# Scores of one pair of heads and values of the pair ahead, issued in one visit of TensorE between the projections

## The chip, the cores and the metric

The kernel runs on one core of one Trainium2 chip. The metric is device time in microseconds (us), the median of three executions. Five engines work side by side, each through its own queue in order: TensorE (PE; its weight loads are shown apart as PEld), VectorE (DVE), ScalarE (ACT), GpSimd (POOL) and SyncE (SP), which issues the DMAs.

## The reference

Two layers over 256 tokens of 1024 channels, float32. Each layer projects the normalised input to queries, keys, values and gates of 16 heads of 64 channels; six heads attend causally, six with a dilated pattern (here a mask and a weight for each pair of tokens), four attend to 256 memory rows; the gated results are projected back and added. Cut to what matters:

```python
def hybrid_layer(x, mem, norm_g, w_in, w_out, mem_norm_g, w_mem_kv, qk_g):
    proj = jnp.einsum('btd,de->bte', rms_norm(x, norm_g), w_in)
    a_q, a_k, a_v, a_g, b_q, b_k, b_v, b_g, m_q, m_g = jnp.split(proj, cuts, axis=-1)
    m_k, m_v = jnp.split(jnp.einsum('bmd,de->bme', rms_norm(mem, mem_norm_g), w_mem_kv), 2, axis=-1)
    oa = moba_attention(rope(rms_norm(a_q)), rope(rms_norm(a_k)), a_v)     # causal, 6 heads
    ob = dilated_attention(rope(rms_norm(b_q)), rope(rms_norm(b_k)), b_v)  # 6 heads
    om = memory_attention(rms_norm(m_q), rms_norm(m_k), m_v)               # 4 heads
    y = jnp.concatenate([oa * jax.nn.silu(a_g), ob * jax.nn.silu(b_g), om * jax.nn.silu(m_g)], axis=-1)
    return x + jnp.einsum('bte,ed->btd', y, w_out)

def memory_attention(q, k, v):
    s = jnp.einsum('bhqd,bhkd->bhqk', q, k) * (HEAD_DIM ** -0.5)
    return jnp.einsum('bhqk,bhkd->bhqd', jax.nn.softmax(s, axis=-1), v)
```

## The kernel before

**Projections.** Every weight is loaded in float32 (`raw`), split into a high part (`hi`, ACT, L449) and a rest (`lo`, DVE, L450), and multiplied by the split input (`xmh`, `xml`) in three products that accumulate in the PSUM tiles `acc` (`products`, L145). The order of a layer is: memory keys and values, memory queries, memory gates; then for the dilated and after it for the causal heads queries, keys, values, gates; then the output projection, whose inputs are the split results `yT0` and `yT1` (tile names with a number: yT_253 is yT0 of layer 0, yT_254 is yT1). A split buffer is free again when the matmuls that read it are done (five buffers), so a late `hi` cast waits for PE.

**Attention of a pair of heads** (`pair_of_heads`, L300, and `head`, L345). Heads go in pairs, eight pairs in a layer: two of memory, three dilated, three causal. A pair passes through these steps on PE, each a short visit between the projections' matmuls:

- four transposes of queries and keys (`wk<-ident,qn`, `wk<-ident,kn`), copied by ACT to `qkT` (L307);
- the scores, `wk<-qkT` (L319): four matmuls in float32 that contract over 64 channels, the two heads in the two halves of the array's rows;
- the softmax off PE: DVE takes the maximum (L351 for memory pairs, L358 with the mask for the others: `nm`, `pr`), ACT the exponentials (L353, L360), DVE the reciprocal (L364), ACT the scaling (L366);
- six or eight transposes of the probabilities (`wk<-ident,pr`, L374), copied by ACT to `pT` (L377);
- the values, `o<-pT,v` (L336): four matmuls that write 64 channels each, the two heads in the two halves of the array's columns;
- then DVE multiplies by the gate (`y`, L341), ACT and DVE split it into `yT0` and `yT1` (L562, L563).

**What sets the order.** The program is written once by Python; PE's order is pinned. Each pair is a generator that yields an estimated delay, and `poll` (L124), which is called between steps of the projections, continues every task whose time has come on an estimated PE clock. Pairs take their scores in order (`live["s"] == me`, L311) and their values in order (`live["v"] == me`, L327); three `wk` tiles and one `o` tile in PSUM are shared. At the output projection `finish` (L136, used in L653) moves the estimated clock on until the result that a step needs has been issued, whatever is or isn't left to put in between. ACT's and DVE's unpinned instructions are placed by the tile framework, which also inserts the semaphores; each engine then goes through its queue in order.

**The end of a layer.** The products of rows e = 1 and 2 of the output projection are held back (L657) and come last, in 24 matmuls that finish one PSUM bank after the other (L663 to L665). Row e = 2 is the last causal pair, the eighth.

Of the kernel before, what the change touches and what calls it, by code (L numbers as in the profile page):

```python
# [10 lines left out]
F32 = mybir.dt.float32  # L11
# [5 lines left out]
P = 128  # L17
T = 256
# [3 lines left out]
HD = 64  # L22
# [9 lines left out]
D_NORM, D_MEM, D_QK, D_SOFTMAX, D_PT, D_EVAC = 8, 1, 2.5, 5, 2.5, 4  # L32
D_FIRST_MEM, D_NEXT_MEM, D_PAIR, D_HEAD = 1, 3, 2, 1
WARM = 7

WHOLE = 2
NEG = -1e30
# [29 lines left out]
def hybrid_kernel(ctx: ExitStack, tc: tile.TileContext, x, mem, mem_t, gains, w_in, w_out, w_mem_kv, qk_g, const, out):  # L67
# [6 lines left out]
    o_p = ctx.enter_context(tc.tile_pool(name="op", bufs=O_BUFS, space=bass.MemoryType.PSUM))  # L74

    def work():
        return wk_p.tile([P, 512], F32, tag="wk", name="wk")
# [22 lines left out]
    clock, tasks = [0.0], []  # L100

    def pe(ins, us):

        tc.keep_in_program_order(ins)
        clock[0] += us

    def mm(out, a, b, start=True, stop=True, shared=False):
        n = b.shape[-1]
        us = 0.02 if shared else max(0.107, n / 2400) if b.dtype == F32R else max(0.214, n / 600)
        pe(nc.tensor.matmul(out, a, b, start=start, stop=stop), us)  # L110

    def transpose(out, a):
        pe(nc.tensor.transpose(out, a, ident), 0.109)  # L113
# [3 lines left out]
    def keep_warm(n):  # L117

        for _ in range(n):
            pe(nc.tensor.matmul(warm[:, 0:P], blank, blank, start=True, stop=True), 0)  # L120

    keep_warm(WARM)

# [9 lines left out]
    def spawn(gen, delay):  # L133
        tasks.append([clock[0] + delay, gen])
# [6 lines left out]
    def until(cond):  # L141
        while not cond():
            yield 0.3
# [125 lines left out]
    def normed(accs, n, dsts, tables, scale=None):  # L269
# [25 lines left out]
                                            op=ALU.mult))  # L295
        return rest

    live = dict(pr=0, pT=0, o=0, heads=0, pairs=0, s=0, t=0, v=0)

    def pair_of_heads(qn, kn, pair, masks, v, gate, ready, finished):  # L300

        ps = work()
        for t in range(NT):
            transpose(ps[:, t * P:(t + 1) * P], qn[:, t, pair * P:(pair + 1) * P])
            transpose(ps[:, 256 + t * P:256 + (t + 1) * P], kn[:, t, pair * P:(pair + 1) * P])
        qkT = sp.tile([P, 2, T], F32, tag="qkT", name="qkT", bufs=SLOTS)
        nc.scalar.copy(qkT.rearrange("p c t -> p (c t)"), ps)  # L307
        me = live["pairs"]
        live["pairs"] += 1
        yield D_QK  # L310
        yield from until(lambda: live["s"] == me and live["pr"] + 2 <= PR_BUFS)  # L311
        live["s"] += 1
        live["pr"] += 2
        scores = [work() for _ in range(2)]
        spans = [slice(0, 2 * P), slice(2 * P, 4 * P)] if masks is None else [slice(0, P), slice(P, 3 * P)]
        for t in range(NT):
            for j in range(2):
                q, k = (qkT[j * HD:(j + 1) * HD, c] for c in range(2))
                mm(scores[j][:, spans[t]], q[:, t * P:(t + 1) * P], k[:, 0:spans[t].stop - spans[t].start])  # L319
        pTs = []  # L320
        for j in range(2):
            rest = head(2 * me + j, scores[j], spans, masks, pTs)
            spawn(rest, next(rest))
        yield D_SOFTMAX
        yield from until(lambda: len(pTs) == 2)
        yield D_PT
        yield from until(lambda: live["v"] == me and live["o"] < O_BUFS and max(ready.values()) <= clock[0])  # L327
        live["v"] += 1
        live["o"] += 1
        o = o_p.tile([P, T], F32, tag="o", name="o")  # L330
        late = slice(0, T) if masks is None else slice(P, T)
        n = 2 * T if masks is None else T + P
        for t, to in ((0, slice(0, T)), (1, late)):
            for j in range(2):
                h = 2 * pair + j
                mm(o[j * HD:(j + 1) * HD, to], v[:, t, h * HD:(h + 1) * HD], pTs[j][:, t * T:n if t else T],  # L336
                   start=t == 0, stop=t == 1, shared=j)
        live["pT"] -= 2
        yield 0.6
        y = sp.tile([P, T], F32, tag="y", name="y", bufs=2)  # L340
        nc.vector.scalar_tensor_tensor(y, o, 0.5, gate[:, pair], op0=ALU.mult, op1=ALU.mult)  # L341
        live["o"] -= 1
        finished(y)
# [50 lines left out]
    for i, (l, c) in enumerate(order):  # L394
        if c in e_rows:
            e0, n = e_rows[c]
            units += [(i, a, min(2, n - a), D) for a in range(0, n, 2)]
        else:
            n = 512 if c == "mkv" else in_cols[c][1]
# [101 lines left out]
    for l in range(DEPTH):  # L501
# [51 lines left out]
        def head_tiles(n, nv):  # L553
            return [sp.tile([P, NT, n], F32, tag=c, name=c, bufs=1) for c in ("qn", "kn")] + [
                sp.tile([P, NT, nv], F32, tag="v", name="v", bufs=2),
                sp.tile([P, n // P, T], F32, tag="gate", name="gate", bufs=2)]
# [3 lines left out]
        def finished(y, e, yT=yT, done=done):  # L560
            done.add(e)
            nc.scalar.copy(yT[0][:, e], y)  # L562
            nc.vector.tensor_tensor(yT[1][:, e], y, yT[0][:, e].bitcast(F32), op=ALU.subtract)  # L563

        def start_heads(pairs, e0, qn, kn, masks, v, gate, ready, delay=D_NORM):
            for pair in range(pairs):
                spawn(pair_of_heads(qn, kn, pair, masks, v, gate, ready,
                                    lambda y, e=e0 + pair: finished(y, e)), delay + D_PAIR * pair)
# [3 lines left out]
        v = kv[:, :, 256:512]  # L572
# [45 lines left out]
        for kind, e0 in ((2, 3), (0, 0)):  # L618
            if kind == 2:
                masks = [cst[:, C_DIL:C_DIL + 128], cst[:, C_DIL + 128:C_DIL + 384]]  # L620
            else:
                masks = [cst[:, C_CAUSAL + 128:C_CAUSAL + 256], cst[:, C_CAUSAL:C_CAUSAL + 256]]
# [3 lines left out]
            qn, kn, v, gate = head_tiles(384, 384)  # L626
# [76 lines left out]
```

## Time and profile before

| | us |
|---|---|
| median of 3 runs (lowest to highest) | 292.39 (292.35 to 293.44) |
| the profiled execution, its own time | 292.14 |
| its span, first to last instruction | 290.3 |
| PE busy in the span | 284.8 (98%) |
| DVE, ACT busy | 205.0, 199.9 |

The page gives PE at 98% of the span and the granted clock of TensorE at 1.00 throughout. The ends of matmuls are modelled and overlap the next, so the reader should go by the distance from one start to the next start, not by the durations. In the section of rows below, "x8" behind the scores or the values are eight hardware matmuls: each float32 matmul of the program is two.

### The profile page before, as it was taken

To read this page: it belongs to the slowest core of one execution; us is meant where nothing else is said; L and a number is where in the kernel's file an instruction comes from. 1 tells how busy PE (TensorE), PEld (TensorE's weight loads), DVE (VectorE), ACT (ScalarE), POOL (GpSimd) and SP (SyncE) were. 2 spreads that over 40 slices of the span, in tenths; PEclk is the share of its full clock that TensorE was granted. 3 is DMA by queue.
4 is the path that set the end of the run, shared out by engine and by line. 5 is a ranking of instruction groups with operands and counts; after the bars stand their busy time and mean duration, and the time that the engine had idled before them with its cause. 6 is when DMAs were issued, how large, how long until landed. Compare 5 with 4: busy or idle time off the path is not lost.

```text
span 290.3 us, 4967 instructions
## 1 busy us (share of the span) xinstructions
PE 284.8 (98%) x1810; PEld 250.0 (86%) x1810; DVE 205.0 (71%) x458; ACT 199.9 (69%) x445; POOL 54.3 (19%) x72
## 2 busy tenths in 40 slices
PE   8999999999999999999999999999999999999994
PEld 5689999889989999877788999989899899987773
DVE  1798999793677996764676577979655699765313
ACT  2899677876789638985366555868578865797600
POOL 0002983210003220000020069503000113000000
PEclk9999999999999999999999999999999999999999
DMA  7999674627335236548025818360913624830003
GB/s 240 377 365 369 216 222 159 167 54 271 111 94 162 72 123 248 213 142 289 3 73 183 255 72 229 135 183 0 325 26 107 232 68 151 310 108 19 3 0 145
DMA packets 32793, 47.33 MB, mean 163 GB/s; under 512 B 1280, under 2 KB 27648, under 8 KB 32768
## 3 DMA queue, kind: packets, MB, share of 16 engines
q1 hardware_dynamic: 32336, 46.22, 48.6%
q10 hardware_dynamic: 432, 0.79, 0.8%
q8 instruction: 14, 0.23, 0.3%
q14 instruction: 11, 0.09, 0.1%
HBM read 45.96 MB, written 1.05 MB: 162 GB/s over the span
## 4 chain that ended last, share of the span: by engine, by line
PE 93%; DMA 3%; DVE 1%; ACT 0%; POOL 0%; SPq 0%; issue 0%; DVEq 0%
PE acc L110 76%; PE wk L113 8%; PE wk L110 5%; PE o L110 5%; DMA x_sb<-in_x_dram 2%; DMA raw<-in_w_mem_kv_dram 1%; DVE xn L491 0%; ACT xn L160 0%; POOL r L155 0%; SPq L428 0%; DVE x_sb L669 0%; SPq L98 0%; DVEq L699 0%; DVE ms L154 0%; PE o L113 0%
## 5 line engine op out<-in xcount | busy, mean ns | idle before, releaser
L450 DVE TENSOR_TENSOR lo<-raw,hi 128x768 fp32r<-128x768 f32 (+1 forms) x91 | 96.8, 1088 | 30.7 <-ACT hi L449 30.7
L449 ACT CAST hi<-raw 128x768 fp32r<-128x768 f32 (+1 forms) x91 | 84.0, 937 | 31.2 <-PE acc L110 21.9
L110 PE MATMUL acc<-hi,xmh 128*128 128x384 f32 (+2 forms) x252 | 67.0, 348 | 0.3 <-ACT hi L449 0.3
L110 PE MATMUL acc<-lo,xmh 128*128 128x384 f32 (+2 forms) x252 | 63.5, 335 | 0.0
L110 PE MATMUL acc<-hi,xml 128*128 128x384 f32 (+2 forms) x252 | 63.5, 335 | 0.0
L155 POOL TENSOR_TENSOR hrs<-ms,mhalf 128x6 f32<-128x6 f32 (+1 forms) x24 | 30.2, 1262 | 118.0 <-DVE ms L154 117.5
L110 PEld LDWEIGHTS acc<-hi,xmh 128*128 128x128 f32 x252 | 42.5, 189 | 5.8 <-issue 3.0
L110 PEld LDWEIGHTS acc<-lo,xmh 128*128 128x128 f32 x252 | 45.0, 188 | 1.2
L110 PEld LDWEIGHTS acc<-hi,xml 128*128 128x128 f32 x252 | 44.9, 188 | 1.2
L110 PE MATMUL acc<-hi,yT 128*128 128x512 f32 x128 | 41.0, 402 | 0.0
L110 PE MATMUL acc<-xmh,hi 128*128 128x256 f32 x128 | 29.7, 293 | 0.0
L110 PE MATMUL acc<-xml,hi 128*128 128x256 f32 x128 | 28.4, 283 | 0.0
L110 PE MATMUL acc<-xmh,lo 128*128 128x256 f32 x128 | 28.3, 283 | 0.0
L110 PEld LDWEIGHTS acc<-hi,yT 128*128 128x128 f32 x128 | 23.0, 188 | 4.8 <-issue 0.7
L360 ACT ACTIVATE pr<-pr,nm 128x128 f32<-128x128 f32 (+1 forms) x48 | 21.3, 446 | 7.7 <-DVE nm L358 7.6
L366 ACT ACTIVATE pr<-pr,rinv 128x128 f32<-128x128 f32 (+1 forms) x64 | 25.8, 462 | 0.0
L110 PE MATMUL acc<-lo,yT 128*128 128x512 f32 x64 | 25.0, 391 | 0.0
L110 PEld LDWEIGHTS acc<-xmh,hi 128*128 128x128 f32 x128 | 20.9, 191 | 0.7 <-issue 0.7
L110 PEld LDWEIGHTS acc<-xml,hi 128*128 128x128 f32 x128 | 21.0, 191 | 0.0
L110 PEld LDWEIGHTS acc<-xmh,lo 128*128 128x128 f32 x128 | 21.0, 191 | 0.0
L377 ACT COPY pT<-wk 128x384 f32<-128x384 f32 (+1 forms) x32 | 15.4, 503 | 6.1 <-PE wk L113 6.1
L358 DVE CUSTOM_DVE_ANT_0 pr<-wk,cst 128x128 f32<-128x128 f32 (+1 forms) x48 | 14.3, 353 | 3.3 <-PE wk L110 3.3
(79 smaller groups left out, 353.1 us busy)
## 6 DMA issues: line engine op xcount, KB each, us to landing
raw<-in_w_in_dram SPq DMA_DIRECT2D x24, 768.0 KB, 5.2
raw<-in_w_in_dram SPq DMA_DIRECT2D x7, 1024.0 KB, 5.8
raw<-in_w_out_dram SPq DMA_DIRECT2D x6, 1024.0 KB, 4.9
raw<-in_w_in_dram SPq DMA_DIRECT2D x6, 512.0 KB, 3.8
raw<-in_w_out_dram SPq DMA_DIRECT2D x4, 512.0 KB, 4.2
raw<-in_w_mem_kv_dram SPq DMA_DIRECT2D x2, 1024.0 KB, 5.1
raw<-in_w_mem_kv_dram SPq DMA_DIRECT2D x2, 512.0 KB, 6.9
x_sb<-in_x_dram SPq DMA_DIRECT2D x2, 512.0 KB, 7.1
```

The lines of the kernel that those rows point to most:

```text
L110: pe(nc.tensor.matmul(out, a, b, start=start, stop=stop), us)
L113: pe(nc.tensor.transpose(out, a, ident), 0.109)
L155: pin(nc.gpsimd.tensor_tensor(dst, ms, mhalf[:, :n], op=ALU.pow))
L358: nc.vector.tensor_tensor_reduce(out=pr[:, spans[t]], in0=s[:, spans[t]], in1=masks[t], scale=-1.0, scalar=3e38, op0=ALU.add, op1=ALU.min, ...
L360: nc.scalar.activation(pr[:, spans[t]], pr[:, spans[t]], AF.Exp, scale=-1.0, bias=nm[:, t:t + 1], accum_out=sums[:, t:t + 1])
L366: nc.scalar.activation(pr[:, spans[t]], pr[:, spans[t]], AF.Copy, scale=rinv[:, t:t + 1])
L377: nc.scalar.copy(pT[:, :n], ps[:, :n])
L449: pin(nc.scalar.copy(hi, raw))
L450: pin(nc.vector.tensor_tensor(lo, raw, hi.bitcast(F32), op=ALU.subtract))
```

## The change

Two waits are added to a pair's generator, and the values are issued from another place.

- A pair with its queries and keys ready no longer takes its scores as soon as two `pr` buffers are free. It waits until the pair ahead has its values ready to issue (or already issued), or until D_PARTNER = 6 us of the estimated clock have gone by.
- When a pair's values are ready, it doesn't issue them: it puts them in `pending`, and waits up to D_SCORES = 3 us for the next pair's scores. The next pair issues its own scores and right behind them the pending values. Otherwise they go alone, as before.

The instructions are the same in kind and number; DMAs and GpSimd's instructions keep their order.

```diff
+D_PARTNER, D_SCORES = 6, 3
...
         yield from until(lambda: live["s"] == me and live["pr"] + 2 <= PR_BUFS)
+        late = clock[0] + D_PARTNER
+        yield from until(lambda: live["v"] >= me or me - 1 in pending or clock[0] >= late)
         live["s"] += 1
...
                 mm(scores[j][:, spans[t]], q[:, t * P:(t + 1) * P], k[:, 0:spans[t].stop - spans[t].start])
         pTs = []
+        if me - 1 in pending:
+            pending.pop(me - 1)()
         for j in range(2):
...
         yield from until(lambda: live["v"] == me and live["o"] < O_BUFS and max(ready.values()) <= clock[0])
-        live["v"] += 1
-        live["o"] += 1
-        o = o_p.tile([P, T], F32, tag="o", name="o")
+        outs = []
+
+        def values():
+            live["v"] += 1
+            live["o"] += 1
+            o = o_p.tile([P, T], F32, tag="o", name="o")
...
+            outs.append(o)
+
+        pending[me] = values
+        late = clock[0] + D_SCORES
+        yield from until(lambda: outs or clock[0] >= late)
+        if not outs:
+            pending.pop(me)()
+        o = outs[0]
```

In the built order seven of a layer's eight pairs have their values right behind the next pair's scores (the eighth has no next pair), and this in both layers. Three places matter below. Line numbers of the changed kernel are higher (L110 becomes L111, L351 L369, L366 L384 and so on).

PE at the end of layer 0, from the eighth pair's probabilities on; before, the transposes of `pr` and the values stand between the output projection's matmuls, and nine of these follow the values ahead of the last 24:

```order
L113 MATMUL wk<-ident,pr 128x128 x3
L110 MATMUL acc<-hi,yT_253 128x512
L110 MATMUL acc<-hi,yT_254 128x512
L110 MATMUL acc<-lo,yT_253 128x512
L113 MATMUL wk<-ident,pr 128x128 x3
...
L110 MATMUL acc<-hi,yT_254 128x512
L110 MATMUL acc<-lo,yT_253 128x512
L110 MATMUL o<-pT,v 64x256 x2
L110 MATMUL o<-pT,v 64x128 x2
L110 MATMUL acc<-hi,yT_253 128x512
```

The same place in the changed kernel, from the eighth pair's scores on (12 matmuls of the output projection stand at the dots):

```order
L111 MATMUL wk<-qkT 128x128 x2
L111 MATMUL wk<-qkT 128x256 x2
L111 MATMUL o<-pT,v 64x256 x2
L111 MATMUL o<-pT,v 64x128 x2
...
L111 MATMUL acc<-lo,yT_253 128x512
L114 MATMUL wk<-ident,pr 128x128 x6
L111 MATMUL o<-pT,v 64x256 x2
L111 MATMUL o<-pT,v 64x128 x2
L111 MATMUL acc<-hi,yT_253 128x512
```

The eighth pair's six transposes and its values now stand directly one behind the other, 12 matmuls behind its scores, and only the last 24 follow.

ACT at the same place of the changed kernel, from the two casts ahead of the eighth pair's exponentials to the split of its result:

```order
L467 CAST hi<-raw 128x1024 x2
L378 ACTIVATE pr,sums<-pr,nm 128x128
...
L384 ACTIVATE pr<-pr,rinv 128x256
L580 CAST yT_253<-y 128x256
L467 CAST hi<-raw 128x1024
L395 COPY pT<-wk 128x384 x2
L580 CAST yT_253<-y 128x256
```

A cast of weights and the seventh pair's `yT` stand between the scaled probabilities and the copies to `pT`; in layer 1 there is no cast there, since no weights are left.

DVE around the second memory pair, layer 0; before, the maxima of its scores (L351) stand ahead of the normalisation of the dilated keys (`hss` to `kn`):

```order
L450 TENSOR_TENSOR lo<-raw,hi 128x768 x4
L351 TENSOR_REDUCE nm<-wk 128x2 x2
L364 RECIPROCAL rinv<-sums 128x2
L341 SCALAR_TENSOR_TENSOR y<-o,gate 128x256
L364 RECIPROCAL rinv<-sums 128x2
L261 TENSOR_REDUCE hss<-sq 128x6
```

In the changed kernel they stand behind it:

```order
L468 TENSOR_TENSOR lo<-raw,hi 128x768 x4
L468 TENSOR_TENSOR lo<-raw,hi 128x1024
L262 TENSOR_REDUCE hss<-sq 128x6
...
L295 TENSOR_TENSOR kn<-t_709,hrs 128x384
L295 TENSOR_TENSOR kn<-t_720,hrs 128x384
L369 TENSOR_REDUCE nm<-wk 128x2 x2
```

The keys' chain and the maxima have changed places on DVE, in layer 1 too.

## Rows read from the trace of the kernel before

**Rows 1.** The page: busy time of the engines; TensorE's granted clock in 40 slices of the span, in tenths (9 is 90% or more); the chain of work that ended last, by engine.
```profile
PE 284.8 (98%) x1810; PEld 250.0 (86%) x1810; DVE 205.0 (71%) x458; ACT 199.9 (69%) x445; POOL 54.3 (19%) x72
...
PEclk9999999999999999999999999999999999999999
...
PE 93%; DMA 3%; DVE 1%; ACT 0%; POOL 0%; SPq 0%; issue 0%; DVEq 0%
```

**Rows 2.** The view of waits, PE alone, the two largest: PE's instructions, who released them, total us, times, longest us.
```profile
PE warm L120 <- DVE mhalf L83: 1.0, 1, 1.0
PE acc L110 <- ACT hi L449: 0.3, 1, 0.3
```

**Rows 3.** The timeline of PE in layer 1: start us, us, engine, line, operation, shapes, count. A visit with a dilated pair's scores alone, then one with a pair's values alone.
```profile
224.82 0.51 PE L110 MATMUL acc<-lo,xmh 128*128 128x384 f32 x2
225.26 0.93 PE L110 MATMUL wk<-qkT 64*128 64x128 f32 x8
226.12 0.62 PE L110 MATMUL acc<-hi,xmh 128*128 128x384 f32 x2
226.58 0.52 PE L110 MATMUL acc<-hi,xml 128*128 128x384 f32 x2
...
227.99 0.51 PE L110 MATMUL acc<-lo,xmh 128*128 128x384 f32 x2
228.43 0.87 PE L110 MATMUL o<-pT,v 128*64 128x256 f32 x8
229.23 0.62 PE L110 MATMUL acc<-hi,xmh 128*128 128x384 f32 x2
229.69 0.51 PE L110 MATMUL acc<-hi,xml 128*128 128x384 f32 x2
```

**Rows 4.** The timeline of PE in layer 0, same columns: a pair's scores with three transposes of another pair's probabilities behind them in the same visit.
```profile
75.61 0.51 PE L110 MATMUL acc<-lo,xmh 128*128 128x384 f32 x2
76.06 0.93 PE L110 MATMUL wk<-qkT 64*128 64x128 f32 x8
...
77.65 0.51 PE L110 MATMUL acc<-hi,xml 128*128 128x384 f32 x2
```

**Rows 5.** The timeline of all engines in layer 0 around the second memory pair: its scores, maxima (L351), exponentials (L353) and scaling (L366), and the first and last instruction of the keys' normalisation on DVE (L261, and L563, which follows it). A releaser stands in brackets with the idle time before.
```profile
49.80 1.13 PE L110 MATMUL wk<-qkT 64*128 64x256 f32 x8
50.87 0.62 PE L110 MATMUL acc<-hi,xmh 128*128 128x384 f32 x2
50.97 1.29 DVE L351 TENSOR_REDUCE nm<-wk 128x2 f32<-128x512 f32 x2 [0.25 <-PE wk L110]
...
51.69 0.47 ACT L353 ACTIVATE pr<-wk,nm 128x256 f32<-128x256 f32 x1 [2.19 <-DVE nm L351]
...
53.06 0.91 ACT L366 ACTIVATE pr<-pr,rinv 128x256 f32<-128x256 f32 x2
...
54.84 0.55 DVE L261 TENSOR_REDUCE hss<-sq 128x6 f32<-128x384 f32 x1 [0.22 <-ACT sq L259]
...
59.64 0.42 DVE L563 TENSOR_TENSOR yT<-y,yT 128x256 fp32r<-128x256 f32 x1
```

**Rows 6.** The timeline of all engines at the end of layer 1, from the eighth pair's scores on: its maxima (DVE L358), exponentials (ACT L360) and scaling (ACT L366); the values of the seventh pair (PE at 270.84) and their way to `y` and `yT`; the eighth pair's transposes and copy; the pace of the output projection.
```profile
266.09 0.93 PE L110 MATMUL wk<-qkT 64*128 64x128 f32 x8
...
267.05 0.29 DVE L358 CUSTOM_DVE_ANT_0 pr<-wk,cst 128x128 f32<-128x128 f32 x1 [0.31 <-PE wk L110]
...
267.38 0.40 ACT L360 ACTIVATE pr<-pr,nm 128x128 f32<-128x128 f32 x1 [0.15 <-DVE nm L358]
...
269.16 0.46 ACT L377 COPY pT<-wk 128x384 f32<-128x384 f32 x1
...
269.52 1.50 ACT L366 ACTIVATE pr<-pr,rinv 128x128 f32<-128x128 f32 x4
...
270.84 0.87 PE L110 MATMUL o<-pT,v 128*64 128x256 f32 x8
270.91 1.04 ACT L449 CAST hi<-raw 128x1024 fp32r<-128x1024 f32 x1
...
271.76 0.42 DVE L341 SCALAR_TENSOR_TENSOR y<-o,gate 128x256 f32<-128x256 f32 x1 [2.23 <-PE o L110]
...
272.22 0.41 ACT L562 CAST yT<-y 128x256 fp32r<-128x256 f32 x1 [0.27 <-DVE y L341]
...
273.17 0.49 PE L113 MATMUL wk<-ident,pr 128*128 128x128 f32 x3
273.41 0.71 PE L110 MATMUL acc<-hi,yT 128*128 128x512 f32 x2
...
273.69 0.48 ACT L377 COPY pT<-wk 128x384 f32<-128x384 f32 x1 [1.07 <-PE wk L113]
273.96 0.40 PE L110 MATMUL acc<-lo,yT 128*128 128x512 f32 x1
...
275.23 0.63 PE L110 MATMUL acc<-hi,yT 128*128 128x512 f32 x2
...
277.27 0.62 PE L110 MATMUL acc<-hi,yT 128*128 128x512 f32 x2
```

**Rows 7.** The timeline of ACT and DVE at the end of layer 0: a cast of weights that PE releases, and the rest that DVE takes behind it.
```profile
137.46 1.05 ACT L449 CAST hi<-raw 128x1024 fp32r<-128x1024 f32 x1 [1.66 <-PE acc L110]
...
138.55 1.23 DVE L450 TENSOR_TENSOR lo<-raw,hi 128x1024 fp32r<-128x1024 f32 x1 [1.87 <-ACT hi L449]
```

More of the change, by code (lines that the diff above doesn't have):

```diff
@@ L296, in normed @@
         return rest
+    pending = {}
     live = dict(pr=0, pT=0, o=0, heads=0, pairs=0, s=0, t=0, v=0)
@@ L327, in pair_of_heads @@
         yield from until(lambda: live["v"] == me and live["o"] < O_BUFS and max(ready.values()) <= clock[0])
-        live["v"] += 1
-        live["o"] += 1
-        o = o_p.tile([P, T], F32, tag="o", name="o")
[L331 to L338, printed above, removed]
+        outs = []
[3 more added lines that the diff above has]
+            o = o_p.tile([P, T], F32, tag="o", name="o")
+            late = slice(0, T) if masks is None else slice(P, T)
+            n = 2 * T if masks is None else T + P
+            for t, to in ((0, slice(0, T)), (1, late)):
+                for j in range(2):
+                    h = 2 * pair + j
+                    mm(o[j * HD:(j + 1) * HD, to], v[:, t, h * HD:(h + 1) * HD], pTs[j][:, t * T:n if t else T],
+                       start=t == 0, stop=t == 1, shared=j)
+            live["pT"] -= 2
+            outs.append(o)
[5 more added lines that the diff above has]
+        o = outs[0]
         yield 0.6
```

## The prediction

> **What bounds the kernel now.** I read the page first. [...] Then the waits of PE, [rows 2]: the two largest are 1.0 and 0.3 us. So PE goes from matmul to matmul, and ACT and DVE cost nothing as long as PE never waits for them. Two things can move the time: the price of the visits themselves, and new waits of PE. I read the first from start to start in the timeline of PE, and the second by following each chain with the durations of the timelines.
>
> The profiled execution is the measure of the sum. Its own time, 292.14, lies 0.25 under the median of 292.39, and I add that at the end.
>
> **What a visit costs.** [Rows 3]: from 226.58 to 227.99 eight projection matmuls pass, 0.175 each. From 224.82 to 226.58 four of them and the scores pass, so the scores cost 1.76 - 0.70 = 1.06. In the same way the values cost 1.70 - 0.70 = 1.00. A visit has three parts. The entry: 225.26 - 224.82 = 0.44 for two matmuls that need 0.35, so 0.09. The body: 0.86 for the scores (225.26 to 226.12), 0.80 for the values. The refill behind it: 226.12 to 226.58 is 0.46 for two matmuls, so 0.11.
>
> **Gain: one visit for two.** Where values stand right behind scores, the refill of the scores and the entry of the values have no projection matmul to fall on: 0.11 + 0.09 = 0.20 saved. No row shows scores followed by values, so I bound it. It may save nothing, if the turn from one kind to the other costs as much as the two turns it replaces. It may save more: the body holds an overhead too. The memory pair's scores, twice as wide in half of their matmuls, have a body of 50.87 - 49.80 = 1.07 against 0.86 [rows 3, 5], so 0.21 for two more blocks of 128 columns, 0.105 a block. Six blocks are 0.63 of useful time in a masked pair, and the values with their total of 1.00 hold about 0.38 beyond that. So each fused visit saves 0 to 0.38, and I take 0.20, the two pieces that rows show by themselves. Seven a layer, 14 in all: -2.8 (0 to -5.3).
>
> **Loss: transposes that had a free ride.** Before, 12 of the visits carry three or four transposes of another pair behind them. [Rows 4]: from 75.61 to 77.65 four matmuls, the scores and three transposes pass, 2.04 - 0.70 = 1.34. Alone, three transposes cost 0.24 (273.17 to 273.41) plus a refill (273.41 to 273.96 is 0.55 for two matmuls of 0.227, so 0.09 or 0.10), 0.33 to 0.34 [rows 6]; 1.06 + 0.335 - 1.34 = 0.055 was saved by each. In the new order only two fused visits carry transposes. Ten lost, by 0.05: +0.5.
>
> **New wait at the second memory pair, both layers.** The pair's scores now stand 24 matmuls, not 6, behind the first pair's transposes, so 18 x 0.174 = 3.1 us later: 49.80 + 3.1 = 52.9 instead of 49.80 [rows 5]. That alone is harmless. But on DVE the maxima have changed places with the keys' normalisation, which takes from 54.84 to 59.64, 4.80 us. Without the two memory visits ahead of it the keys' last product ends about 2.3 us earlier; a cast and its rest (1.05 and 1.23 as in [rows 7]) that PE releases at about 50.6 stand in front of it on DVE, so it begins at about 50.6 + 1.1 + 1.15 = 52.85. It ends at 57.65. From the maxima to the first exponential are 0.72 (50.97 to 51.69), to 58.4; four exponentials take 0.46 each (51.69 to 53.06 is three), to 60.2. ACT has another pair's `yT` (0.41) and `qkT` (0.59 in the estimate) in front of the scaling, to 61.1; the scaling of a head is 0.91, and PE can go on at about 61.9. PE wants these transposes at 52.9 + 1.07 (scores) + 1.01 (values) + 0.11 + 24 x 0.174 + 0.44 (four transposes of queries) + 6 x 0.174 + 0.1 = 60.85. So it waits about 1.05, and 2.1 in both layers. Bounds: 0 if the normalisation starts 1.1 earlier than I have it, 1.3 if the cast is later. What is queued behind the maxima on DVE (the first pair's `y`) has time.
>
> **The end of layer 1.** Zero is the start of the eighth pair's scores; durations by [rows 6]. Scores 0.86, the seventh pair's values 0.80, refill 0.11, then 12 matmuls of the output projection at (277.27 - 275.23)/9 = 0.227, 2.7: PE wants the eighth pair's transposes at 4.5. The maxima start at 0.96, the exponentials run from 1.29 to 3.07 (267.38 to 269.16), the scaling ends 1.39 (269.52 to 270.91) later, 4.46: just in time. But before, 12 matmuls stood between the transposes and the values, and now none. The first copy to `pT` begins 0.52 behind the transposes (273.17 to 273.69), the second 0.36 later (269.16 to 269.52 is the pitch) and takes 0.46: 4.5 + 0.52 + 0.36 + 0.46 = 5.85. The values count from about 5.9 and end at 6.7; without the wait they would have ended at 4.5 + 0.66 (six transposes, twice the 0.33 above) + 0.09 + 0.80 = 6.06. That is 0.66. Then the last 24 matmuls begin at once, where before nine others covered the way through `y` and `yT`. With S = the end of the values' body, `y` begins at S + 0.12 (271.76 against 270.84 + 0.80), `yT0` at S + 0.58 (272.22), it ends at S + 0.99 and `yT1` at S + 1.45. PE has three matmuls of row e = 1, to S + 0.80, and then needs `yT0`, one matmul later `yT1`: 0.24 and 0.23. Together 1.13.
>
> **The end of layer 0.** The same, with casts of the next layer's weights among it. A cast that PE releases just ahead of the eighth scores sends its rest (1.23, [rows 7]) to DVE in front of the maxima, which start at 2.15 instead of 0.96; the scaling ends at 5.7. Then ACT has the seventh pair's `yT` (0.41) and another cast (1.0) in front of the copies: 5.7 + 0.41 + 1.0 + 0.36 + 0.46 = 7.9. The first matmul of the values needs only the first copy, so they count from 7.8 and end at 8.6, 2.5 behind 6.06. With the same 0.47 behind them: 3.0. If both casts turn out later or earlier than the copies, it is 1.13 as in layer 1; if the last cast waits for PE, it can be 4.
>
> **The sum.** -2.8 + 0.5 + 2.1 + 3.0 + 1.1 = +3.9; 292.14 + 3.9 + 0.25 = 296.3.
>
> **Rivals.** *The waits are hidden* (not slower). The place is the order of the casts and the keys' normalisation: if the normalisation ends 1.1 earlier, the second memory pair waits for nothing, and if the casts miss the last pair of layer 0, its end costs 1.13. Then -2.8 + 0.5 + 2 x 1.13 = 0, 292.4; it decides as soon as all waits together stay under 2.3. For it: [rows 5, 7] show ACT with idle time ahead of its work, 2.19 and 1.66. Against it: in the new order the copies come directly in front of the values in both layers, and nothing can move between. Chance 0.17.
>
> *The turn from scores to values is free.* The whole overhead of the values falls, -5.3 + 0.5 + 6.2, 293.8. Rows can't exclude it, but every change of kind that they show has a price. [...] Chance 0.10.
>
> *The visit saves nothing.* The turn costs what the two outer ones did: 0 + 0.5 + 6.2, 299.1. Chance 0.08.
>
> *The clock falls.* [...] [Rows 1, 2] show 1.00 in all slices with waits of 1.0 at most, and no wait of 2.5 to read it from. [...] Chance 0.05.
>
> **How the numbers follow.** The forecast has 0.60, with its own range of 294.0 to 298.5. 0.5% is 1.46 us, about what a measurement of this kernel can tell from no change. Faster by that much comes only from the hidden waits with more than 0.20 saved a visit: 0.06. Within it: the rest of that rival (0.11), half of the free turn (0.05), and the low edge of the forecast (0.03): 0.19. Slower: 0.75. The range takes the forecast, the free turn, the visit that saves nothing, and part of the hidden waits: 292.6 to 299.4.
>
> **What would show it.** In the timeline of PE, a fused visit should have 0.86 from the first score to the first value, 0.80 from there to the next matmul, and no gap; 1.06 and 1.00 would speak for the visit that saves nothing, 0.6 for the free turn. In the waits, PE should stand for the scaling of `pr` about 1 us at each layer's second memory pair, for ACT's `pT` about 2.5 in layer 0 and 0.6 in layer 1, and for `yT` about 0.5 at each end; the chain should pass through ACT and DVE there. I am wrong if PE's waits sum to less than 4 or more than 9, if the clock leaves 1.00, or if PE waits in the middle of a layer.

## The result

Six runs of each kernel give 296.55 us (296.2 to 297.3) for the changed kernel and 293.07 (292.35 to 293.79) for the one before: a ratio of 1.0129, with a 95% interval of 1.0112 to 1.0145. It is 1.3% slower.

The page of the changed kernel: busy time; the granted clock in 40 slices; the chain of work that ended last, by engine.

```profile
PE 285.5 (97%) x1810; PEld 250.8 (85%) x1810; DVE 205.1 (70%) x458; ACT 199.9 (68%) x445; POOL 54.2 (18%) x72
...
PEclk9999999999999999999999999999999999999999
...
PE 85%; ACT 6%; DVE 5%; DMA 2%; issue 1%; SPq 0%; DVEq 0%; ACTq 0%
```

Against [rows 1], no engine has less or more to do, and the granted clock is 9 in every slice again, with a mean of 1.00. What has changed is the chain: PE's share is 85% instead of 93%, and ACT and DVE, which had 0% and 1%, have 6% and 5%. PE's busy time tells little: it is 285.5 instead of 284.8, while the span is 4.5 longer.

The view of waits of the changed kernel, PE alone (total us, times, longest):

```profile
PE o L111 <- ACT pT L395: 1.4, 2, 1.2
PE wk L114 <- ACT pr L384: 1.2, 2, 0.6
...
PE acc L111 <- ACT hi L467: 0.8, 1, 0.8
```

[Rows 2] had only the waits at the start. The two on top are new, and this view shows too little of them: it counts idle time from the modelled end of the matmul ahead, and it has none of the waits inside a group of transposes, which are shown below. So the sizes are read from start to start.

**A measure that leaves the start out.** The profiled execution of the changed kernel took 296.62, 4.5 more than that of before, the medians differ by 3.5. The code up to the first transposes of queries is the same in both, but they begin at 36.24 us before and at 36.85 here (in the experiments between 36.20 and 37.05): the first loads landed at other times in these two executions (the three of `memT` took 5.0 us from issue to landing before and 6.0 here, by median), and PE waited shorter or longer for the first casts (0.3 in [rows 2], 0.8 here). From these transposes on, equal code repeats itself to some hundredths: the transposes of the second memory pair's probabilities come 25.28 behind them in the changed kernel (62.13) and in the experiments tail_apart and cast_late, 25.32 in cover6, all four with the same order on PE up to there. So I use two distances between starts in the timeline of PE: layer 0, from the first transposes of queries (`wk<-ident,qn`) to the first transposes of layer 1's input (`wk<-ident,xn`); layer 1, from there to the last matmul. Each is read from one profiled execution of its kernel.

| kernel | time, us | ratio to before (95%) | layer 0 | layer 1 | sum |
|---|---|---|---|---|---|
| before | 293.07 | | 117.29 | 132.75 | 250.04 |
| changed | 296.55 | 1.0129 (1.0112 to 1.0145) | 120.02 | 133.91 | 253.93 |
| gap | 300.10 | 1.0253 (1.0224 to 1.0281) | 121.88 | 135.90 | 257.78 |
| early_first | 294.04 | 1.0059 (1.0041 to 1.0078) | 118.88 | 132.71 | 251.60 |
| tail_apart | 294.03 | 1.0056 (1.0037 to 1.0076) | 118.39 | 133.48 | 251.87 |
| cast_late | 296.37 | 1.0121 (1.0093 to 1.0149) | 119.63 | 133.91 | 253.54 |
| cover6 | 294.38 | 1.0067 (1.005 to 1.0085) | 118.99 | 132.73 | 251.72 |
| early_cover6 | 291.90 | 0.9985 (0.997 to 0.9999) | 117.79 | 131.59 | 249.39 |
| early_apart67 | 292.17 | 0.9993 (0.9978 to 1.0008) | 117.27 | 132.31 | 249.59 |
| mix | 290.23 | 0.9918 (0.99 to 0.9935) | 116.56 | 131.55 | 248.11 |
| reverse (one run) | 292.82 | | 117.94 | 132.00 | 249.93 |

The experiments' ratios are to runs of the kernel before on the same chip (medians 292.37, 292.41 and 292.49), not to the 293.07 of the first row. By this measure the change costs 3.89, 2.73 of it in layer 0 and 1.16 in layer 1.

**A fused visit.** The timeline of PE, changed kernel, layer 1, the place of [rows 3]:

```profile
225.23 0.51 PE L111 MATMUL acc<-lo,xmh 128*128 128x384 f32 x2
225.68 0.93 PE L111 MATMUL wk<-qkT 64*128 64x128 f32 x8
226.53 0.87 PE L111 MATMUL o<-pT,v 128*64 128x256 f32 x8
227.33 0.62 PE L111 MATMUL acc<-hi,xmh 128*128 128x384 f32 x2
227.79 0.51 PE L111 MATMUL acc<-hi,xml 128*128 128x384 f32 x2
```

From 225.23 to 227.79 four projection matmuls and the visit pass: 2.56 - 0.70 = 1.86, where scores and values apart cost 1.06 and 1.00. The bodies are what they were, 0.85 to 0.86 from the first score to the first value and 0.80 from there; one entry and one refill are gone, 0.20. Fourteen times, this is 2.8.

**The second memory pair, layer 0.** The timeline of all engines, changed kernel, the place of [rows 5]:

```profile
53.44 0.55 DVE L262 TENSOR_REDUCE hss<-sq 128x6 f32<-128x384 f32 x1
...
53.54 1.13 PE L111 MATMUL wk<-qkT 64*128 64x256 f32 x8
...
57.30 1.02 DVE L295 TENSOR_TENSOR kn<-t,hrs 128x384 f32<-128x384 f32 x2
...
58.23 1.28 DVE L369 TENSOR_REDUCE nm<-wk 128x2 f32<-128x512 f32 x2
...
58.95 0.47 ACT L371 ACTIVATE pr<-wk,nm 128x256 f32<-128x256 f32 x1 [0.24 <-DVE nm L369]
...
60.77 0.41 ACT L580 CAST yT<-y 128x256 fp32r<-128x256 f32 x1
...
61.02 0.51 PE L111 MATMUL acc<-lo,xmh 128*128 128x384 f32 x2
...
61.54 1.72 ACT L384 ACTIVATE pr<-pr,rinv 128x256 f32<-128x256 f32 x4
...
62.13 0.94 PE L114 MATMUL wk<-ident,pr 128*128 128x128 f32 x4 [0.60 <-ACT pr L384]
...
62.83 0.59 PE L111 MATMUL acc<-hi,xmh 128*128 128x384 f32 x2
```

The scores start at 53.54, but the maxima (L369) only at 58.23, behind the keys' normalisation (`hss` to `kn`); in [rows 5] they started 1.17 behind the scores. PE is through with its projection matmuls at 61.02 + 0.35 = 61.37 and starts the transposes at 62.13, after the first scaling; the four take 0.70 to 62.83, where the four of the queries and keys at 59.89 take 0.35, since the second needs the next scaling: its weight load at 62.53 stands 0.26 for it. PE stands for 0.76 + 0.35 = 1.11, of which the brackets tell 0.60. Ahead of the scaling ACT has another pair's `yT` and `qkT`, from 60.77 to 61.54. Layer 1 has the same.

**The end of layer 1.** Same view, the place of [rows 6]:

```profile
278.10 0.93 PE L111 MATMUL wk<-qkT 64*128 64x128 f32 x8
...
279.06 0.29 DVE L376 CUSTOM_DVE_ANT_0 pr<-wk,cst 128x128 f32<-128x128 f32 x1 [4.89 <-PE wk L111]
...
282.62 0.82 PE L114 MATMUL wk<-ident,pr 128*128 128x128 f32 x6
...
283.15 0.86 ACT L395 COPY pT<-wk 128x384 f32<-128x384 f32 x2 [0.21 <-PE wk L114]
...
283.68 1.25 PE L111 MATMUL o<-pT,v 128*64 128x256 f32 x8 [0.24 <-ACT pT L395]
...
284.85 0.72 PE L111 MATMUL acc<-hi,yT 128*128 128x512 f32 x2
...
285.86 0.42 DVE L581 TENSOR_TENSOR yT<-y,yT 128x256 fp32r<-128x256 f32 x1 [0.47 <-ACT yT L580]
...
285.88 0.95 PE L111 MATMUL acc<-hi,yT 128*128 128x512 f32 x2
...
286.67 0.39 PE L111 MATMUL acc<-lo,yT 128*128 128x512 f32 x1
```

The transposes start at 282.62 without a wait, the copies at 283.15, the values at 283.68. From 282.62 to 284.85 are 2.23; six transposes with a refill (0.66), an entry (0.09) and the values (0.80) need 1.55, so PE stands 0.68, for the copies to `pT`. Then from 284.85 to 286.67 five matmuls take 1.82, where the first five behind the same values take 1.28 in the timeline of the kernel before: 0.54 for `yT`.

```profile
278.85 0.74 PE L110 MATMUL acc<-hi,yT 128*128 128x512 f32 x2
...
280.13 0.39 PE L110 MATMUL acc<-lo,yT 128*128 128x512 f32 x1
```

**The end of layer 0.** Same view, the place of [rows 7]:

```profile
135.28 1.04 ACT L467 CAST hi<-raw 128x1024 fp32r<-128x1024 f32 x1 [1.68 <-PE acc L111]
...
135.40 0.93 PE L111 MATMUL wk<-qkT 64*128 64x128 f32 x8
...
136.36 1.23 DVE L468 TENSOR_TENSOR lo<-raw,hi 128x1024 fp32r<-128x1024 f32 x1 [1.50 <-PE wk L111]
...
137.50 0.28 DVE L376 CUSTOM_DVE_ANT_0 pr<-wk,cst 128x128 f32<-128x128 f32 x1
...
139.60 1.48 ACT L384 ACTIVATE pr<-pr,rinv 128x128 f32<-128x128 f32 x4
...
140.04 1.53 PE L114 MATMUL wk<-ident,pr 128*128 128x128 f32 x6
...
140.98 0.39 ACT L580 CAST yT<-y 128x256 fp32r<-128x256 f32 x1
...
141.28 1.04 ACT L467 CAST hi<-raw 128x1024 fp32r<-128x1024 f32 x1
...
142.23 0.84 ACT L395 COPY pT<-wk 128x384 f32<-128x384 f32 x2
...
142.75 1.24 PE L111 MATMUL o<-pT,v 128*64 128x256 f32 x8 [1.18 <-ACT pT L395]
...
143.92 0.73 PE L111 MATMUL acc<-hi,yT 128*128 128x512 f32 x2
...
145.73 0.40 PE L111 MATMUL acc<-lo,yT 128*128 128x512 f32 x1
```

A cast at 135.28 sends its rest to DVE (L468, 136.36), and the maxima come at 137.50, 2.10 behind the scores instead of the 0.96 of layer 1. The scaling ends at 141.08, `yT` and the next cast follow, the copies come at 142.23 and end at 143.07. From 140.04 to 143.92 are 3.88, with 0.12 more ahead of the transposes: against 1.55, PE stands 2.45. For `yT` it stands 0.53 here (143.92 to 145.73 is 1.81).

### The profile page after: what moved, and what is told of

Its sections match the earlier page's. It is cut to its first block, busy times and chain, and to the rows that moved or that the text cites. A ratio compares the mean times of both kernels' runs of the same rounds, so it can differ in the third digit from the quotient of the medians.

```text
span 294.8 us, 4984 instructions
## 1 busy us (share of the span) xinstructions
PE 285.5 (97%) x1810; PEld 250.8 (85%) x1810; DVE 205.1 (70%) x458; ACT 199.9 (68%) x445; POOL 54.2 (18%) x72
## 3 DMA queue, kind: packets, MB, share of 16 engines
HBM read 45.96 MB, written 1.05 MB: 159 GB/s over the span
## 4 chain that ended last, share of the span: by engine, by line
PE 85%; ACT 6%; DVE 5%; DMA 2%; issue 1%; SPq 0%; DVEq 0%; ACTq 0%
PE acc L111 70%; PE wk L114 7%; PE wk L111 4%; PE o L111 4%; DMA memT<-in_mem_t_dram 2%; ACT hi L467 1%; ACT pr L371 1%; DVE lo L468 1%; ACT pr L384 1%; DVE t L281 1%; DVE hss L262 1%; DVE sq L285 1%; ACT yT L580 1%; ACT pr L378 1%; DVE kn L295 0%
## 5 line engine op out<-in xcount | busy, mean ns | idle before, releaser
L468 DVE TENSOR_TENSOR lo<-raw,hi 128x768 fp32r<-128x768 f32 (+1 forms) x91 | 97.2, 1089 | 38.4 <-ACT hi L467 35.9
L111 PE MATMUL acc<-hi,xmh 128*128 128x384 f32 (+2 forms) x252 | 66.3, 346 | 0.8 <-ACT hi L467 0.8
L111 PE MATMUL acc<-lo,xmh 128*128 128x384 f32 (+2 forms) x252 | 63.5, 335 | 0.0
L111 PE MATMUL acc<-hi,xml 128*128 128x384 f32 (+2 forms) x252 | 63.5, 334 | 0.0
L111 PEld LDWEIGHTS acc<-hi,xmh 128*128 128x128 f32 x252 | 42.8, 189 | 4.6 <-issue 1.8
L111 PEld LDWEIGHTS acc<-lo,xmh 128*128 128x128 f32 x252 | 45.0, 188 | 1.2
L111 PEld LDWEIGHTS acc<-hi,xml 128*128 128x128 f32 x252 | 44.9, 188 | 1.1
L111 PE MATMUL acc<-hi,yT 128*128 128x512 f32 x128 | 41.5, 404 | 0.1
L111 PE MATMUL acc<-xmh,hi 128*128 128x256 f32 x128 | 29.6, 292 | 0.0
L111 PEld LDWEIGHTS acc<-hi,yT 128*128 128x128 f32 x128 | 23.0, 188 | 6.5 <-issue 1.0
L111 PE MATMUL acc<-xmh,lo 128*128 128x256 f32 x128 | 28.4, 283 | 0.0
L111 PE MATMUL acc<-xml,hi 128*128 128x256 f32 x128 | 28.3, 282 | 0.0
L384 ACT ACTIVATE pr<-pr,rinv 128x128 f32<-128x128 f32 (+1 forms) x64 | 25.3, 461 | 0.0
L111 PE MATMUL acc<-lo,yT 128*128 128x512 f32 x64 | 25.0, 391 | 0.0
L111 PEld LDWEIGHTS acc<-xmh,hi 128*128 128x128 f32 x128 | 20.9, 191 | 0.8 <-issue 0.8
L111 PEld LDWEIGHTS acc<-xmh,lo 128*128 128x128 f32 x128 | 21.0, 191 | 0.0
L111 PEld LDWEIGHTS acc<-xml,hi 128*128 128x128 f32 x128 | 21.0, 191 | 0.0
```

The lines of the kernel that those rows point to most:

```text
L384: nc.scalar.activation(pr[:, spans[t]], pr[:, spans[t]], AF.Copy, scale=rinv[:, t:t + 1])
L468: pin(nc.vector.tensor_tensor(lo, raw, hi.bitcast(F32), op=ALU.subtract))
```

## The experiments

**gap**: the values at the next step of the projections, 3 or 6 matmuls behind the scores.

```diff
         if me - 1 in pending:
-            pending.pop(me - 1)()
+            def then():
+                if me - 1 in pending:
+                    pending.pop(me - 1)()
+                yield 0
+            spawn(then(), 0)
```

> The changed kernel, but the values are issued at the next step of the projections behind the scores (3 or 6 matmuls later) instead of directly behind them; pairs are otherwise taken as in the changed kernel, with the same two waits. It measures the visit's price with nearly the same waits. Theory (a fused visit saves the refill of the scores and the entry of the values): 14 x 0.205 = 2.9 more, less 0.1 for joints with transposes, 299.3; the scores cost 1.06 and the values 1.00 again. Rival (putting them behind one another saves nothing, and only waits have changed): 296.5. A third case, that the waits shrink with the step between: 298.

300.10, and the sum rises by 3.85. The visits cost 1.06 and 1.00 again. The wait at the second memory pair grows, by 0.54 in each layer (the transposes behind it take 1.64 longer than without a wait, 1.10 in the changed kernel), and the wait at the end of layer 0 is 0.2 shorter: 3.85 - 1.08 + 0.2 = 2.97 for 14 visits, 0.21 each. So the fusing itself is a gain, and of the size that was expected; the rival falls.

**early_first**: the first pair's values are ready 2 us earlier on the estimated clock.

```diff
-        yield D_PT
+        yield 0.5 if me % 8 == 0 else D_PT
```

> The changed kernel, but the first memory pair's values are ready 2 us of the estimated clock earlier, so that the first fused visit of a layer stands 12 matmuls behind the first pair's transposes, not 24; on DVE the second pair's maxima then stand ahead of the keys' normalisation. All 14 fused visits stay. Theory (the second memory pair waits because its maxima stand behind the normalisation): both waits of 1.1 go and two visits more carry transposes, 2.3 less than the changed kernel, 294.3, and no wait of PE for the scaling of pr. Rival (the wait is that of ACT behind yT and qkT, whatever DVE does, or it moves to the dilated pair behind): 296.0 or more, with waits of the same sum at a neighbouring place.

294.04, the sum falls by 2.33, and PE no longer waits for the scaling at the second memory pairs (at the end of layer 0 it still does). The timeline of DVE and ACT, second memory pair of layer 0:

```profile
52.98 1.28 DVE L369 TENSOR_REDUCE nm<-wk 128x2 f32<-128x512 f32 x2
...
54.18 0.54 DVE L262 TENSOR_REDUCE hss<-sq 128x6 f32<-128x384 f32 x1
...
57.26 0.93 ACT L384 ACTIVATE pr<-pr,rinv 128x256 f32<-128x256 f32 x2
```

The maxima (L369) are ahead of `hss` now, the scaling (L384) ends at 58.2, and the transposes need it at 59.45. With the maxima first the wait is gone. But the edit moves more than that order: from the pair's scores to its transposes PE now has 8.44 of work instead of 7.83, and `yT` and `qkT`, which took 0.77 in front of the scaling, come behind it. Each of these two is smaller than the wait of 1.11, while the maxima were 3.5 late (4.69 behind the scores instead of 1.17). So the order on DVE is much the largest of the three; no run moves it alone.

**tail_apart**: the eighth pair doesn't wait, and the seventh's values don't either.

```diff
-        late = clock[0] + D_PARTNER
+        late = clock[0] + (0 if me % 8 in (7,) else D_PARTNER)
...
-        late = clock[0] + D_SCORES
+        late = clock[0] + (0 if (me + 1) % 8 in (7,) else D_SCORES)
```

> The changed kernel, but the eighth pair doesn't wait for the seventh, and the seventh pair's values don't wait for the eighth's scores; both go alone, as before the change, in both layers. Six fused visits a layer stay. Theory (the loss comes from waits that a lack of work between steps makes): the ends give back 2.45 and 0.68 of PE's standing for the copies and about 0.5 each for yT, 4.1; two fused visits lost cost 0.4 and two regained joints with transposes give 0.1, so 3.8 less than the changed kernel, 292.8, and no wait of PE for pT or yT at either layer's end. Rival (the fused visits themselves cost the time, by the turn from scores to values): 0.3 less, 296.3, with the chain still on PE.

294.03, the sum falls by 2.06 where 3.8 was expected. The wait for `pT` is gone at both ends, as expected. The wait for `yT` is not: the eighth pair has become late by the visits ahead of it, its values still stand directly ahead of the last 24 matmuls, and PE stands 0.54 in layer 1 as in the changed kernel, and in layer 0 1.1, since the rest of a cast now comes in front of `yT1` on DVE. So 2.45 + 0.68 gained, 0.3 for two fused visits and their joints (the free ride of transposes directly behind a visit) and 0.6 for `yT` in layer 0 lost: 2.2. The expectation had taken the end of before for granted, which the edit doesn't bring back.

**cast_late**: at the end of layer 0 the copies of the eighth pair stand ahead of the cast on ACT; PE's order is the same, and on DVE the eighth pair's `y` now stands ahead of the cast's rest.

```diff
                     last.append((e, w))
+                    if e == 1:
+                        finish(lambda: live["t"] == 16 * (l + 1))
                     continue
```

> The changed kernel, but at the end of each layer the eighth pair's transposes and copies are written ahead of the next split of weights; PE's order is the same, and on ACT one row moves: the copies to pT of the eighth pair in layer 0 stand ahead of a cast of weights instead of behind it. Theory (the cast's 1.0 is in the way of the copies): PE's wait for pT in layer 0 shrinks by 1.0, 295.5. Rival (the copies come late by the chain in front, the scaling and yT, and the cast runs in time that is lost anyway; or the late cast delays the next layer's first matmuls as much): within 0.3 of the changed kernel.

296.37: its ratio can't be told from that of the changed kernel. Layer 0 is 0.39 shorter. The timeline of all engines there:

```profile
140.23 1.53 PE L114 MATMUL wk<-ident,pr 128*128 128x128 f32 x6
...
141.47 0.84 ACT L395 COPY pT<-wk 128x384 f32<-128x384 f32 x2
...
141.99 1.24 PE L111 MATMUL o<-pT,v 128*64 128x256 f32 x8 [0.23 <-ACT pT L395]
...
143.60 1.22 DVE L468 TENSOR_TENSOR lo<-raw,hi 128x1024 fp32r<-128x1024 f32 x1
...
144.74 0.42 DVE L581 TENSOR_TENSOR yT<-y,yT 128x256 fp32r<-128x256 f32 x1
...
145.21 0.50 PE L111 MATMUL acc<-hi,yT 128*128 128x512 f32 x1 [0.53 <-DVE yT L581]
```

The copies start 1.24 behind the transposes instead of 2.19, and from the transposes to the values are 1.76 instead of 2.71: 0.95 gained, as expected. But counted from the transposes the cast comes 0.7 later and its rest 1.1, so that the rest (L468, 143.60) is now in front of `yT1` (144.74) on DVE, and PE stands 0.58 longer for it, ahead of 145.21. What was gained at one place of the queues comes back at the next, 0.58 of 0.95.

**cover6**: six held-back matmuls between the eighth pair's transposes and values, six more behind the values.

```diff
+                if e == 2:
+                    for part in whole_banks[:2]:
+                        out_products(1, last[0][1], *part)
                 finish(lambda: e in done)
...
                     last.append((e, w))
+                    if e == 1:
+                        finish(lambda: live["t"] == 16 * (l + 1))
                     continue
...
+        for part in whole_banks[2:]:
+            out_products(1, last[0][1], *part)
         for t, c, n in whole_banks:
-            for e, w in last:
+            for e, w in last[1:]:
```

> The changed kernel with all 14 fused visits, but at the end of each layer six of the held-back matmuls (row e = 1, first two banks) are issued between the eighth pair's transposes and its values, and the other six of that row between the values and row e = 2; the copies to pT stand ahead of the cast in layer 0. Theory (PE stands at the ends because nothing is left to put between transposes, copies, values and yT): the wait for the copies goes in layer 1 (0.68) and in layer 0 down to what the scaling costs, about 1.0 of 2.45, and the 0.46 for yT goes at both ends: from the first transposes of queries to the last matmul 3.0 less than the changed kernel, 251.0 us, and the time 293.6. Rival (the ends are bound by the eighth pair's chain from scores to yT, and matmuls put between only move the standing behind them): less than 1 gained, 295.6 or more.

294.38, the sum falls by 2.21 where 3.0 was expected. Layer 1 gives 1.18, nearly all of its 0.68 and 0.54; but this kernel ends 4.27 behind its last matmul, the changed one 4.05, and the sum leaves these 0.22 out. Layer 0 gives 1.03 of the 1.9 expected. The eighth pair's waits for `pT` and `yT` are gone. Its six transposes, with the first matmuls behind them, still cost 1.85 instead of 0.66: of these 1.19, about 0.94 is the wait for the scaling (1.0 was expected), and 0.25 is one for the seventh pair's `yT1`, which DVE finishes at 141.23 and the second of the held-back matmuls needs. And the step from row e = 2 to layer 1's first products takes 1.32 (147.48 to 148.80), where the changed kernel takes 0.67 (149.84 to 150.51). The timeline of all engines there:

```profile
145.99 1.23 DVE L468 TENSOR_TENSOR lo<-raw,hi 128x1024 fp32r<-128x1024 f32 x1 [1.02 <-ACT hi L467]
...
147.13 2.48 DVE L694 TENSOR_TENSOR x_sb<-acc,x_sb 128x512 f32<-128x512 f32 x4
...
147.86 0.19 PEld L111 LDWEIGHTS acc<-hi,xmh 128*128 128x128 f32 x1 [0.41 <-DVE x_sb L694]
```

With row e = 2 alone at the end, a bank is finished every three matmuls instead of every six. DVE reads out the four banks one right behind the other (L694), and only when the rest of a cast (L468) is done; layer 1's first products wait for a bank to be read out, the weight load at 147.86 for 0.41. Of the 0.87 that are missing in layer 0, about 0.1 stays open.

**early_cover6**: early_first and cover6 together.

> The two mends together: the first pair's values early, as in early_first, and six matmuls between the steps of the eighth pair, as in cover6; 14 fused visits. Theory (the fused visits are a gain of 2.9 less 0.4 for joints, and all of the loss is the four places of waits): 5.2 less than the changed kernel from the first transposes of queries to the last matmul, 248.7 us against 250.0 of the kernel before, and a time 1.3 to 1.5 below the kernel before, ratio 0.995. Rival (waits come back elsewhere once these are gone): no faster than the kernel before.

291.90, ratio 0.9985; the sum is 0.65 below the kernel before where 1.3 was expected. Layer 1 is 1.16 below, which is 7 x 0.205 less 0.27, most of it for joints (four lost): with no wait left inside it, the fused visits show their gain. Behind the last matmul it loses 0.21, as in cover6, which the sum leaves out. Layer 0 is 0.50 above, with 1.2 for the scaling and `yT1`, and 0.68 at layer 1's first products (1.35 instead of 0.67), as in cover6.

**early_apart67**: early_first, and in both layers the seventh and eighth pairs apart (as tail_apart, with 6 and 7).

> The first pair's values early, and the seventh and eighth pairs take scores and values apart, as before the change, so that five of a layer's visits are fused and the end of a layer is as in the kernel before. Theory: ten fused visits save 2.05, joints lose 0.1, and no wait is left at the second memory pair or at the ends: 248.1 us from the first transposes of queries to the last matmul, 1.9 below the kernel before, ratio 0.993. Rival (waits come back elsewhere): no faster than the kernel before.

292.17, ratio 0.9993 with 1 inside its interval. The sum is 249.59 where 248.1 was expected: `yT` costs 0.54 in layer 1 and 1.1 in layer 0 again, 1.6, and I had expected none, by the same mistake as in tail_apart.

**mix**: the first pair early in both layers. Layer 0: the seventh and eighth pairs apart, row e = 1 of two banks behind the eighth's values. Layer 1: all fused, row e = 1 of one bank between transposes and values, of two behind them.

```diff
...
+        rows = [(1, 1), (1, 2), (2, 0), (2, 1), (2, 2), (1, 3), (2, 3)] if l else [
+            (1, 0), (1, 1), (2, 0), (2, 1), (1, 2), (2, 2), (1, 3), (2, 3)]
+        for r, b in rows:
+            t, c, n = whole_banks[b]
+            out_products(r, last[r - 1][1], t, c, n)
...
```

> The first pair's values early in both layers. Layer 0: the seventh and eighth pairs apart, and behind the eighth's values six matmuls of row e = 1 ahead of row e = 2, so that yT has 1.4 us of cover. Layer 1: all fused, three matmuls of row e = 1 between the eighth pair's transposes and values, six behind them. Twelve fused visits. Theory: layer 0 falls from the 117.3 of early_apart67 by the 1.03 that PE stood for yT, to 116.3; layer 1 is the 131.6 of early_cover6; 247.9 us from the first transposes of queries to the last matmul, 2.1 less than the kernel before, ratio 0.993. Rival (the standing in layer 0 moves on to the next layer's first products, which wait for the casts and for the banks to be read out): 248.9, ratio 0.9965.

290.23, ratio 0.9918 (0.99 to 0.9935): faster than both kernels. The sum is 248.11 where 247.9 was expected. In its view of waits, PE waits for neither `pr` nor `pT`; beside waits in the first 17 us it has one, what is left of the 1.1 for `yT` in layer 0 (about 0.4 from start to start):

```profile
PE acc L111 <- DVE yT L581: 0.2, 1, 0.2
```

The kernel before has no such waits [rows 2]: there the new order of row e = 1 and the earlier values had nothing to win by themselves, and so far as the rows tell, mix is faster by its visits. These edits were not tried without fused visits.

**reverse**: early_cover6 with the values first and the scores behind them.

> As early_cover6, but in a fused visit the values of the pair ahead come first and the scores of the next pair right behind them, 14 times. It asks whether the saving belongs to the turn from scores to values or to there being one visit for two. Theory (one entry and one refill are saved, whatever comes first): the visit of a masked pair costs 1.85 to 1.87, as in the other order. Rival (the turn has a price of its own, and another from values to scores): a visit that differs by 0.1 or more, 1.4 us over 14. The scores come 0.8 to 1.0 later, which may bring waits at the ends; those are told apart in the rows.

The timeline of PE, layer 1, a masked pair:

```profile
221.36 0.87 PE L111 MATMUL o<-pT,v 128*64 128x256 f32 x8
222.16 0.93 PE L111 MATMUL wk<-qkT 64*128 64x128 f32 x8
223.01 0.62 PE L111 MATMUL acc<-hi,xmh 128*128 128x384 f32 x2
```

0.80 and 0.85, and with 0.10 for the entry and 0.11 for the refill a visit of 1.86 as in the other order. The saving belongs to there being one visit for two. The scores come later by the values ahead of them, and at the ends PE waits for the scaling again: the eighth pair's six transposes cost 1.79 and 1.17 there, 0.66 without a wait.

## Why the prediction was right, point by point

**The gain of a visit** was taken as 0.20 out of 0 to 0.38. The rows give 0.20, gap 0.21. The free turn is refuted: the body of the values is 0.80 behind the scores as it is alone. From the first score to the first value are 0.85 or 0.86, as many as from the first score to a projection matmul in [rows 3], 0.86. So the values behind the scores start as late as a projection matmul there, and nothing of the bodies is saved.

**The joints with transposes** were taken at 0.05 each, ten lost. The one fused visit of each layer that carries transposes agrees: it costs 2.24, where a visit alone costs 1.86 and four transposes 0.44.

**The second memory pair** was to wait 1.05 and waits 1.11. Counted from the pair's scores, the maxima were to start at 4.75 and start at 4.69, the first exponential at 5.5 and starts at 5.41. early_first, with the maxima ahead of the keys' normalisation, has no wait there. By the rows the order on DVE is the main cause, though no run moved it alone.

**The end of layer 1**: the values were to end 6.7 behind the eighth pair's scores and end at 6.75 (278.10 to 284.85); the standing was to be 0.66 and is 0.68. **The end of layer 0**: the maxima at 2.15 (2.10), the scaling's end at 5.7 (5.68), the second copy's end at 7.9 (7.67), the values' end at 8.6 (8.52), the standing 2.5 (2.45). Here two small misses cancel, which is luck: the copies end 0.2 earlier than forecast, and the values end 0.85 behind the second copy instead of 0.7, since their second matmul needs the second copy. **For `yT`** 0.47 was expected at each end, and 0.54 and 0.53 are measured: the sum left out that the matmul behind such a wait takes 0.34 to the next start (286.33 to 286.67) instead of 0.23, 0.11 more, as much as a refill.

**The sum** was +3.9, and the distance is +3.89. That they agree to a hundredth is luck, as is some of the agreement between 296.3 and 296.55: the forecast stood on 292.39, the median of three runs, while six give 293.07. By the measured terms: -2.9 for the visits, +0.5 for joints, 2.2, 0.68 + 2.45, and 1.1 make +4.0 to +4.1. The difference, 0.1 to 0.2, is about the size of one oddity in the trace of before: one visit of scores there takes 1.04 from its first score to the next matmul (85.31 to 86.35) where the others take 0.86, with no cause that the rows show. early_first took one term away and left the others as they were, cover6 took away those of layer 1. That the rest of a cast ahead of the maxima in layer 0 is worth about 1.1 was read from rows alone: moving it wasn't tried by itself. PE's waits sum to 6.4, between the 4 and 9 of the forecast.

**The clock** stayed at 1.00 while PE stood 2.45 us within 4 at the end of layer 0, so that rival fell here. Its chance of 0.05 was my estimate; what a lower clock costs, no run shows, since the mean granted clock of the profiled executions is 0.997 to 1.00. **The hidden waits** are out too: all three places are there.

**Where expectations failed**: twice, in tail_apart and early_apart67, the wait for `yT` was forgotten, because I thought of the end of a layer as restored when only the order of two pairs was. And in cast_late, cover6 and early_cover6 part of a gain in layer 0 came back as a new wait, on DVE or in the next layer.

## What to carry to other kernels

Merging two visits of a saturated engine saved one entry and one refill here, 0.20 us, and the price can be read beforehand from start to start around each; look then for what the merging moves on the other engines, since a step that comes 3 us later can land behind 5 us of other work in a queue. Where nothing is left to issue between the steps of a chain, keep some independent work back for just that place: here 14 fused visits cost 1.3% without such work; 12 of them, with it and with the first pair's values early, gained 0.8%. Compare executions from a point behind the first loads when less than a microsecond matters.

## What was not expected of the hardware

The order of the two kinds of matmul in a visit made no difference here: 1.86 for scores ahead of values and for values ahead of scores. And the start of the same code moved by up to 0.85 us between executions (first transposes of queries from 36.20 to 37.05), while what follows keeps its distances: layer 1 takes 133.91 in the changed kernel and 133.91 again in cast_late, whose layer 1 has the same order.
